# Eight experts in two interleaved streams: wide and narrow experts block by block in turn, instead of one after the other

## The chip, the cores and the metric

The kernel runs on one core of a Trainium2 chip. The metric is the device time of one execution in microseconds, the median of several runs. Beside it stands one profiled execution, whose trace all rows below come from.

## What is computed

The kernel is a two-layer backbone: layer 0 is a state-space and retention mixer with a dense feed-forward part, layer 1 is differential attention and a mixture of eight experts, of which each of the 256 tokens uses two. The change touches the experts alone:

```
def swiglu(h, w_gate, w_up, w_down):
    return (jax.nn.silu(h @ w_gate) * (h @ w_up)) @ w_down

def moe(h, w_router, w_gate, w_up, w_down):
    logits = (h @ w_router).astype(jnp.float32)
    top_val, top_idx = lax.top_k(logits, TOP_K)
    top_w = jax.nn.softmax(top_val, axis=-1)
    combine = jnp.sum(jax.nn.one_hot(top_idx, N_EXPERTS, dtype=jnp.float32) * top_w[..., None], axis=-2)
    out = jnp.zeros_like(h)
    for e in range(N_EXPERTS):
        out = out + combine[..., e:e + 1].astype(h.dtype) * swiglu(h, w_gate[e], w_up[e], w_down[e])
    return out
...
xl = xl + g2 * moe(hl, odd_router[j], odd_exp_gate[j], odd_exp_up[j], odd_exp_down[j])
```

The model width is 1024, an expert's inner width 3584, all in float32. One expert has 3 x 1024 x 3584 weights, 44 MB; the eight have 352 MB, and each weight is read once.

## The kernel before, in words

The experts are sorted by how many tokens chose them. The first four places have 128 token slots each and are called wide here; the last four have 64 slots and are called narrow (`SLOTS`). Tokens that fit nowhere would be done in a conditional part behind them, which this input doesn't enter. `ORDER` runs the places one whole expert at a time, wide and narrow in turn: 0, 7, 1, 6, 2, 5, 3, 4.

A *unit* is one weight transfer of 1 MiB (128 partitions x 2048 float32). An expert has 28 units of gate and up (seven blocks of 512 inner columns, four units each) and 14 units of down. `raw2` issues them on SP's queue in the order of the code, into a ring: two units go into four small buffers of 512 KB, the following ones into large tiles of two units each (`self.wide` lists the tiles: four of them before). A large tile is free again when both of its units have been used.

A **wide expert** (`expert`) splits each weight tile into a rounded part and a remainder: `wsplit` lets ScalarE make `hi` (L183) and VectorE make `lo` (L184), with three buffers of each, and each product is three matmuls (L194 to L196) on the whole 128x128 array. After each block come silu (L1493), the product with up (L1495), four transposes on TensorE (L1498), and the split of the result into `ah` and `al` (L1500, L1501). Its combine back to the tokens is L1522 and L1523.

A **narrow expert** (`expert_half`) multiplies the weights in plain float32, with no split. Its 64 slots fill half of the array's columns, and two halves of the weights' columns run side by side (L1443 gate and up, L1457 down; each such matmul has two records in the trace). After each block come silu (L1446), the product (L1448), and `turn`: two transposes (L1425) and a copy (L1426), which the code puts ahead of the third unit of the next block. Its end is a copy of the result scaled by the token's weight (L1465) and the combine (L1470).

`gather` fetches the slots of the next expert by matmuls with a selection matrix (L1357 and around), in the middle of the expert before it. `values_load` (L1245) reads the number of the expert at a place into a register of SP, since the address of its weights depends on it. In the last expert, a narrow one, the row of output gates (`row`, L357) and four partial sums on POOL (`so_far`, L1408 and L1409) are made, and `put` adds the last products and writes out.

The order on each engine is laid out when the program is built: a planner takes the instructions by their place in the code and by when it expects their operands and buffers. So an engine's order needn't be that of the code; at run time each engine keeps the order that it was given.

Of the kernel before, what the change touches and what calls it, by code (L numbers as in the profile page):

```python
# [10 lines left out]
F32 = mybir.dt.float32  # L11
# [8 lines left out]
P = 128  # L20
D = 1024
# [7 lines left out]

ORDER = (0, 7, 1, 6, 2, 5, 3, 4)  # L30
SLOTS = (CAP,) * 4 + (HALF,) * 4
# [108 lines left out]
class Net:  # L140
# [33 lines left out]
    def wraw(self, ap):  # L174
        t = self.pw.tile([P, 1024], F32, name="raw", tag="raw", bufs=5)
        self.nc.sync.dma_start(t, ap)
        return t
# [985 lines left out]
class Layer1Experts(Layer1):  # L1163
# [72 lines left out]
    def experts(self):  # L1236
        nc = self.nc
        v = nc.vector
        self.nraw, self.wide, self.al_slot, self.rest_slot = -5, (2, 3, 0, 1), 4, 4
        self.place, self.eid = self.rank, [0] * NE  # L1240
        g = self.gather(0, 0)
        self.sorted()
        for i, n in enumerate(ORDER):
            if n:
                self.eid[n] = nc.values_load(self.ids[0:1, n:n + 1], engines=[mybir.EngineType.SP],  # L1245
                                             min_val=0, max_val=NE - 1)
            nxt = ORDER[i + 1] if i + 1 < NE else None
            run = self.expert if SLOTS[n] == CAP else self.expert_half
            g = run(n, g, 0, nxt, not i, nxt is None)

        more = nc.values_load(self.more[0:1, 0:1], min_val=0, max_val=256)
        with self.tc.If(more > 0):
            self.nraw, self.wide, self.al_slot = 0, (3, 0, 1), 2
            for t in range(2):
                v.memset(self.moe[:, t, :], 0.0)
            for n in range(NE):
                extra = nc.values_load(self.extra[0:1, n:n + 1], min_val=-P, max_val=256)
                with self.tc.If(extra > 0):
                    self.expert(n, self.gather(n, SLOTS[n]), SLOTS[n], None, False, False)
# [69 lines left out]
    def gather(self, n, base):  # L1329
# [18 lines left out]
        for t in range(2):  # L1348
            nc.scalar.activation(pn[:, t, 0:w], p[:, t, 0:w], AF.Copy, scale=self.rs2[:, t:t + 1])
        xg = self.scr("q8", (P, KD, w)) if half else self.scr("q8", (P, 2, KD, P), F32R)  # L1350
        per = 512 // w
# [20 lines left out]
        for t in range(2):  # L1372
            nc.tensor.matmul(pt[:, 256:257], p[:, t, :], wts[:, t, n:n + 1], start=t == 0, stop=t == 1)
        pT = self.scr("m1", (P, 256), F32 if half else F32R)
        nc.scalar.activation(pT, pt[:, 0:256], AF.Copy)
        wt = self.scr("gw", (P, 1))
        v.tensor_copy(wt, pt[:, 256:257])
        return xg, pT, wt

    def raw2(self, ap):  # L1380
# [13 lines left out]
        self.nc.sync.dma_start(t.rearrange("p u c -> p (u c)"), ap)  # L1394
        return [t[:, i] for i in range(2)]
# [14 lines left out]

    def expert_half(self, n, gathered, base, nxt, first, final):

# [4 lines left out]
        sides = [slice(HALF * i, HALF * i + HALF) for i in range(2)]  # L1417
        if final:
            self.rest = self.big(self.rest_slot, (P, 3, D), name="rest")
            self.row("odd", 5, 0, self.rest[:, 2])  # L1420
        ap = self.big(5, (P, FE // P, HALF), name="ef")
        def turn(b, t):
# [7 lines left out]
        for b in range(FE // 512):  # L1430
            if final and 2 <= b < 6:
                self.so_far(b - 2)
# [27 lines left out]
        if final:  # L1460
# [5 lines left out]
        for t in range(2):  # L1466
            for j, s in enumerate(sides):
# [5 lines left out]
                else:  # L1473
                    v.tensor_tensor(self.moe[:, t, c], self.moe[:, t, c], pt, op=ALU.add)
        return out

    def expert(self, n, gathered, base, nxt, first, final):
        nc = self.nc
        v = nc.vector
        xg, pT, w_tok = gathered  # L1480
        ah = self.big(5, (P, FE // P, P), F32R, "eh")
        al = self.big(self.al_slot, (P, FE // P, P), F32R, "el")
        for b in range(FE // 512):
            pg, pu = self.mm(2 * (b % 2)), self.mm(2 * (b % 2) + 1)
            for u in range(0, KD, 2):
                raw = self.raw2(self.weights("exp_gu", n, b, u // 2))
                for i in range(2):
                    hi, lo = self.wsplit(raw[i])
# [6 lines left out]
            v.tensor_tensor(t, sg, pu, op=ALU.mult)  # L1495
            pt = self.tr()
            for f in range(4):
                nc.tensor.transpose(pt[:, P * f:P * f + P], t[:, P * f:P * f + P], self.ident)  # L1498
            p3 = pt.rearrange("p (f s) -> p f s", f=4)
            nc.scalar.activation(ah[:, 4 * b:4 * b + 4, :], p3, AF.Copy)  # L1500
            v.tensor_tensor(al[:, 4 * b:4 * b + 4, :], p3, ah[:, 4 * b:4 * b + 4, :].bitcast(F32), op=ALU.subtract)  # L1501
        out = self.gather(nxt, base) if nxt is not None else None
        py = [self.acc(), self.acc()]
        nd = FE // P
        for u in range(0, nd, 2):
# [3 lines left out]
            for f, j in sorted(steps, key=lambda s: s[1]) if u == nd - 2 else steps:  # L1509
                hi, lo = w[f - u]  # L1510
                c = slice(512 * j, 512 * j + 512)
                self.mm3(py[j], ah[:, f, :], al[:, f, :], hi[:, c], lo[:, c], f == 0, f == nd - 1)
        for j in range(2):
            c = slice(512 * j, 512 * j + 512)
# [4 lines left out]
            for t in range(2):  # L1519
# [4 lines left out]
                m = self.moe[:, t, c]  # L1524
                if first:
                    v.tensor_copy(m, pt)
                else:
                    v.tensor_tensor(m, m, pt, op=ALU.add)
        return out

# [18 lines left out]
```

## Time and profile before

| | us |
|---|---|
| median of 3 runs (2022.72 to 2029.66) | 2026.68 |
| the profiled execution | 2025.02 |
| span of its instructions | 2023.2 |
| first matmul of the first expert, from the span's start | 1120.5 |
| last weights landed | 2008.1 |

The profiled execution's own time is 1.8 us over its span. Times in the rows are microseconds from the span's start; a matmul's end is modelled, so the start of the next one says when it was done. PE is TensorE, PEld its weight loads, DVE VectorE, ACT ScalarE, POOL GpSimd and SP the engine whose queue issues the transfers. An idle time in brackets is that of the engine just before the instruction, with what ended it.

### The profile page before, as it was taken

The page shows a single profiled execution, that of the slowest core. Times are in us where ns is not written, and L with a number is a line of the kernel's source. Part 1 is how long each engine was busy: PE and PEld are TensorE (multiplying, and loading weights), DVE is VectorE, ACT ScalarE, POOL GpSimd, SP SyncE. Part 2 cuts the span into 40 slices and gives each one's busy share as a digit, 9 for nine tenths or more (in the row PEclk, how much of TensorE's full clock was granted, in tenths as well). Part 3 has the DMA queues.
Part 4 walks back from the last instruction along what each step waited for, and adds up shares of the span by engine and source line. Part 5 has one row for each costly group of instructions (what it writes and reads, how often), then busy time and mean ns, then how long its engine had stood idle before and what let it go on. Part 6 is the DMA issues. An engine that isn't in the chain of part 4 may idle for free.

```text
span 2023.2 us, 26554 instructions
## 1 busy us (share of the span) xinstructions
PE 1943.0 (96%) x9894; PEld 1440.6 (71%) x9894; DVE 1225.9 (61%) x2105; ACT 906.3 (45%) x1373; POOL 10.1 (1%) x12
## 2 busy tenths in 40 slices
PE   7999999999999999999989999999999999999997
PEld 4776778777888888877857887548854786558752
DVE  5568578745866565578566886049811984059700
ACT  5535346533333213245365774148712773158610
POOL 0000000000000000000000000000000000000010
PEclk9999999999999999999989999999999999999999
DMA  8333434442555554424325489999999999999897
GB/s 321 111 94 106 145 115 146 141 135 80 201 178 173 177 178 172 144 87 126 107 99 219 165 326 359 417 418 417 348 394 418 417 361 360 417 418 412 326 394 314
DMA packets 103865, 502.68 MB, mean 248 GB/s; under 512 B 13104, under 2 KB 13744, under 8 KB 69296
## 3 DMA queue, kind: packets, MB, share of 16 engines
q1 hardware_dynamic: 103728, 500.91, 66.0%
q8 instruction: 80, 1.31, 0.3%
q14 instruction: 57, 0.47, 0.1%
HBM read 495.62 MB, written 5.24 MB: 248 GB/s over the span
## 4 chain that ended last, share of the span: by engine, by line
PE 82%; DMA 7%; DVE 7%; ACT 3%; issue 1%; SPq 0%; ACTq 0%; DVEq 0%
PE mm L196 17%; PE mm L195 17%; PE mm L194 17%; PE mm L1443 9%; DMA wide<-exp_d 4%; PE acc L195 2%; PE acc L196 2%; PE acc L194 2%; DVE lo L184 2%; PE tr L1357 1%; PE acc L315 1%; PE acc L1457 1%; PE tr L1470 1%; PE mm L1138 1%; PE tr L817 1%
## 5 line engine op out<-in xcount | busy, mean ns | idle before, releaser
L183 ACT ACTIVATE hi<-raw 128x1024 fp32r<-128x1024 f32 x224 | 237.3, 1060 | 410.6 <-PE mm L196 204.7
L184 DVE TENSOR_TENSOR lo<-raw,hi 128x1024 fp32r<-128x1024 f32 x224 | 273.1, 1222 | 176.6 <-ACT hi L183 169.4
L184 DVE TENSOR_TENSOR lo<-wide,hi 128x1024 fp32r<-128x1024 f32 x268 | 324.7, 1223 | 34.8 <-ACT hi L183 14.1
L183 ACT ACTIVATE hi<-wide 128x1024 fp32r<-128x1024 f32 x268 | 282.5, 1061 | 75.2 <-PE mm L196 52.6
L195 PE MATMUL mm<-lo,q 128*128 128x512 f32 x448 | 177.8, 397 | 2.0 <-DVE lo L184 1.7
L196 PE MATMUL mm<-hi,q 128*128 128x512 f32 x448 | 176.0, 393 | 0.0
L194 PE MATMUL mm<-hi,hh 128*128 128x512 f32 x416 | 169.0, 407 | 1.7 <-DVE b L856 1.3
L1443 PE MATMUL mm<-wide,q 128*64 128x256 f32 x1424 | 168.7, 382 | 0.0
L195 PE MATMUL mm<-lo,hh 128*128 128x512 f32 x416 | 164.9, 396 | 0.0
L196 PE MATMUL mm<-hi,hl 128*128 128x512 f32 x416 | 163.9, 396 | 0.0
L194 PE MATMUL mm<-hi,q 128*128 128x512 f32 x448 | 159.1, 395 | 0.0
L194 PE MATMUL mm<-h2h,hi 128*128 128x512 f32 (+1 forms) x376 | 142.5, 379 | 1.3 <-ACT hi L183 1.3
L195 PE MATMUL mm<-h2l,hi 128*128 128x512 f32 (+1 forms) x376 | 141.9, 377 | 0.0
L196 PE MATMUL mm<-h2h,lo 128*128 128x512 f32 (+1 forms) x376 | 141.8, 378 | 0.0
L1443 PEld LDWEIGHTS mm<-wide,q 128*64 128x64 f32 x1424 | 100.3, 137 | 55.1 <-issue 8.1
L1448 DVE TENSOR_TENSOR s<-s,mm 128x256 f32<-128x256 f32 x28 | 11.8, 421 | 184.7 <-ACT s L1446 184.7
L195 PEld LDWEIGHTS mm<-lo,q 128*128 128x128 f32 x448 | 84.9, 190 | 24.1 <-DVE lo L184 4.1
L194 PEld LDWEIGHTS mm<-hi,q 128*128 128x128 f32 x448 | 84.5, 189 | 23.9 <-issue 4.5
L194 PEld LDWEIGHTS mm<-hi,hh 128*128 128x128 f32 x416 | 78.4, 189 | 27.8 <-issue 9.7
L196 PEld LDWEIGHTS mm<-hi,q 128*128 128x128 f32 x448 | 84.8, 189 | 16.9
L1457 PE MATMUL acc<-wide,ef 128*64 128x512 f32 x360 | 82.4, 598 | 11.0 <-DMA wide<-exp_d 11.0
L196 PEld LDWEIGHTS mm<-hi,hl 128*128 128x128 f32 x416 | 78.5, 189 | 17.1 <-issue 0.8
(393 smaller groups left out, 3319.7 us busy)
## 6 DMA issues: line engine op xcount, KB each, us to landing
wide<-exp_gu SPq DMA_DIRECT2D x177, 1024.0 KB, 10.4
wide<-exp_d SPq DMA_DIRECT2D x91, 1024.0 KB, 11.6
raw<-exp_gu SPq DMA_DIRECT2D x92, 512.0 KB, 12.5
raw<-odd_wmod SPq DMA_DIRECT2D x48, 512.0 KB, 4.0
raw<-w_in SPq DMA_DIRECT2D x44, 512.0 KB, 3.7
raw<-ffn_gu SPq DMA_DIRECT2D x44, 512.0 KB, 4.4
raw<-exp_d SPq DMA_DIRECT2D x42, 512.0 KB, 14.7
raw<-even_wmod SPq DMA_DIRECT2D x36, 512.0 KB, 3.7
```

Of the source, the lines that this page charges most:

```text
L183: nc.scalar.activation(hi, raw, AF.Copy)
L184: nc.vector.tensor_tensor(lo, raw, hi.bitcast(F32), op=ALU.subtract)
L194: mm(ps, lh, rh, start=first, stop=False, skip_group_check=skip)
L195: mm(ps, lh, rl, start=False, stop=False, skip_group_check=skip)
L196: mm(ps, ll, rh, start=False, stop=last, skip_group_check=skip)
L315: nc.tensor.matmul(ps[r:r + 32, :], self.cond[:, k, :], raw[:, 512 * kk:512 * kk + 512], start=k < 4, stop=k >= 4)
L817: nc.tensor.matmul(pe, m, r.rearrange("p h l -> p (h l)"), start=d + i == 0, stop=d + i == 2)
L1138: nc.tensor.matmul(ps, self.qT1[r, h, qs], self.kT1[r, h, :], start=True, stop=True)
L1357: nc.tensor.matmul(pt[:, w * kk:w * kk + w], self.x[:, 2 + t, P * (k + kk):P * (k + kk) + P], pn[:, t, 0:w], start=t == 0, stop=t == 1)
L1443: mm(ps[s, 256 * g:256 * g + 256], xg[:, k, :], raw[i][:, c:c + 256], start=k + g == 0, stop=k == KD - 1, skip_group_check=True)
L1457: mm(py[s], ap[:, f, :], raw[f - u][:, 512 * j:512 * j + 512], start=f == 0, stop=f == nd - 1, skip_group_check=True)
L1470: mm(pt, pT[s, P * t:P * t + P], y[s], start=True, stop=True)
```

## The change

`ORDER` goes. The wide places 0 to 3 and the narrow places 4 to 7 become two generators that yield after each block of gate and up and after each two units of down, 14 times an expert (`STEPS`). The wide stream runs three steps alone (`LEAD`), and then each loop turn asks one step of the wide and one of the narrow stream. The narrow stream gets operands of its own (`ef`, `xgh`, `pTs`) in the large tile 1, which leaves the ring: `self.wide` has three tiles instead of four. The narrow stream uses the PSUM banks 2 and 3, the wide stream 0 and 1 (and all four in its first three blocks). The narrow `turn` goes ahead of the second unit of its next block instead of the third; the wide transposes get a `turn` too, ahead of the second unit of the next block instead of right behind their own. The loads of expert numbers are ordered behind the weight transfer issued last. The gate row and the partial sums of the output come behind the wide stream's end.

```
-ORDER = (0, 7, 1, 6, 2, 5, 3, 4)
+STEPS, LEAD = 14, 3
...
     def wraw(self, ap):
-        self.nc.sync.dma_start(t, ap)
+        self.loaded = self.nc.sync.dma_start(t, ap)
...
     def experts(self):
-        self.nraw, self.wide, self.al_slot, self.rest_slot = -5, (2, 3, 0, 1), 4, 4
+        self.nraw, self.wide, self.al_slot, self.rest_slot = -5, (2, 3, 0), 4, 4
+        nb = self.big(1, name="nb")
+        self.ef = nb[:, 0:1792].rearrange("p (f s) -> p f s", s=HALF)
+        self.xgh = nb[:, 1792:2304].rearrange("p (k s) -> p k s", s=HALF)
+        self.pTs = [nb[:, 2304 + 256 * i:2560 + 256 * i] for i in range(2)]
         self.place, self.eid = self.rank, [0] * NE
         g = self.gather(0, 0)
         self.sorted()
-        for i, n in enumerate(ORDER):
-            if n:
-                self.eid[n] = nc.values_load(self.ids[0:1, n:n + 1], engines=[mybir.EngineType.SP],
-                                             min_val=0, max_val=NE - 1)
-            nxt = ORDER[i + 1] if i + 1 < NE else None
-            run = self.expert if SLOTS[n] == CAP else self.expert_half
-            g = run(n, g, 0, nxt, not i, nxt is None)
+        wide = [n for n in range(NE) if SLOTS[n] == CAP]
+        narrow = [n for n in range(NE) if SLOTS[n] == HALF]
+
+        def stream(run, ns, g):
+            for i, n in enumerate(ns):
+                if n:
+
+                    with self.tc.issue_after(self.loaded.ins):
+                        self.eid[n] = nc.values_load(self.ids[0:1, n:n + 1], engines=[mybir.EngineType.SP],
+                                                     min_val=0, max_val=NE - 1)
+                g = yield from run(n, g, ns[i + 1] if i + 1 < len(ns) else None, n == NE - 1)
+
+
+        full = stream(self.expert, wide, g)
+        for _ in range(LEAD):
+            next(full)
+        half = stream(self.expert_half, narrow, self.gather(narrow[0], 0))
+        for _ in range(STEPS * len(wide) - LEAD):
+            next(full)
+            next(half)
+        drain(full)
+        self.rest = self.big(self.rest_slot, (P, 3, D), name="rest")
+        self.row("odd", 5, 0, self.rest[:, 2])
+        for b in range(4):
+            self.so_far(b)
+        drain(half)
...
     def gather
-        xg = self.scr("q8", (P, KD, w)) if half else self.scr("q8", (P, 2, KD, P), F32R)
+        xg = self.xgh if half else self.scr("q8", (P, 2, KD, P), F32R)
...
-        pT = self.scr("m1", (P, 256), F32 if half else F32R)
+        pT = self.pTs[n % 2] if half else self.scr("m1", (P, 256), F32R)
...
     def expert_half
-            ps = self.mm(b % 4)
+            ps = self.mm(2 + b % 2)
             for u in range(0, KD, 2):
                 raw = self.raw2(self.weights("exp_gu", n, b, u // 2))
-                if t is not None and u == 4:
+                if t is not None and u == 2:
                     turn(b - 1, t)
...
             v.tensor_tensor(t, sg, ps[:, 256:512], op=ALU.mult)
-        out = self.gather(nxt, base) if nxt is not None else None
+            yield
         turn(FE // 512 - 1, t)
-        py = self.acc()
+        out = self.gather(nxt, 0) if nxt is not None else None
+        py = self.mm(3)
...
+            if u % 4 == 2 and u < nd - 2:
+                yield
...
     def expert
+        def turn(b, t):
+            pt = self.tr()
+            for f in range(4):
+                nc.tensor.transpose(pt[:, P * f:P * f + P], t[:, P * f:P * f + P], self.ident)
+            p3 = pt.rearrange("p (f s) -> p f s", f=4)
+            nc.scalar.activation(ah[:, 4 * b:4 * b + 4, :], p3, AF.Copy)
+            v.tensor_tensor(al[:, 4 * b:4 * b + 4, :], p3, ah[:, 4 * b:4 * b + 4, :].bitcast(F32), op=ALU.subtract)
+
+        t = None
         for b in range(FE // 512):
-            pg, pu = self.mm(2 * (b % 2)), self.mm(2 * (b % 2) + 1)
+
+            i0 = 2 * (b % 2) if not n and b < LEAD else 0
+            pg, pu = self.mm(i0), self.mm(i0 + 1)
             for u in range(0, KD, 2):
                 raw = self.raw2(self.weights("exp_gu", n, b, u // 2))
+                if t is not None and u == 2:
+                    turn(b - 1, t)
...
-            pt = self.tr()
-            for f in range(4):
-                nc.tensor.transpose(pt[:, P * f:P * f + P], t[:, P * f:P * f + P], self.ident)
-            p3 = pt.rearrange("p (f s) -> p f s", f=4)
-            nc.scalar.activation(ah[:, 4 * b:4 * b + 4, :], p3, AF.Copy)
-            v.tensor_tensor(al[:, 4 * b:4 * b + 4, :], p3, ah[:, 4 * b:4 * b + 4, :].bitcast(F32), op=ALU.subtract)
-        out = self.gather(nxt, base) if nxt is not None else None
+            yield
+        turn(FE // 512 - 1, t)
+        out = self.gather(nxt, 0) if nxt is not None else None
```

## Rows read from the trace of the kernel before

**Rows 1.** The page, part 1: busy time, share of the span, instructions.

```profile
PE 1943.0 (96%) x9894; PEld 1440.6 (71%) x9894; DVE 1225.9 (61%) x2105; ACT 906.3 (45%) x1373; POOL 10.1 (1%) x12
```

**Rows 2.** Table by stretches: length, busy time (instructions) by engine, clock, DMA share, GB/s.

```profile
1564.60:1691.20 126.60, 126.09 (x574) 102.39 (x573) 110.07 (x103) 94.63 (x105) 0.00 (x0) 0.99 0.97 388
1691.20:1789.50 98.30, 90.39 (x627) 47.20 (x626) 11.03 (x21) 15.35 (x35) 0.00 (x0) 1.00 0.98 397
...
1135.50:2008.10 872.60, 835.73 (x4672) 576.87 (x4672) 465.80 (x471) 422.48 (x530) 9.93 (x8) 1.00 0.97 386
...
1560.00:1580.00 20.00, 18.86 (x63) 11.80 (x62) 14.31 (x15) 12.51 (x14) 0.00 (x0) 0.91 1.02 418
1580.00:1600.00 20.00, 19.63 (x91) 15.91 (x90) 18.43 (x19) 15.39 (x18) 0.00 (x0) 1.00 1.01 418
```

**Rows 3.** Line 1457 in four stretches (as rows 2); then TensorE's timeline, one of them.

```profile
1308.16:1337.54 29.38, 25.80 (x112) 7.41 (x112) 1.00 1.01 417
1534.52:1560.43 25.91, 24.48 (x112) 7.82 (x112) 1.00 1.02 417
1759.76:1785.51 25.75, 24.69 (x112) 7.85 (x112) 1.00 1.02 417
1980.65:2011.81 31.16, 26.01 (x112) 7.49 (x112) 1.00 0.89 366
...
1759.76 12.24 PE L1457 MATMUL acc<-wide,ef 128*64 128x512 f32 x56
1771.82 3.60 PE L1457 MATMUL acc<-raw,ef 128*64 128x512 f32 x16
```

**Rows 4.** TensorE's timeline from 1565: start, length, line, operation, count, idle before.

```profile
1565.15 0.63 PE L195 MATMUL mm<-lo,q 128*128 128x512 f32 x1
1565.57 0.63 PE L196 MATMUL mm<-hi,q 128*128 128x512 f32 x1
1566.00 0.63 PE L195 MATMUL mm<-lo,q 128*128 128x512 f32 x1
...
1567.42 0.40 PE L196 MATMUL mm<-hi,q 128*128 128x512 f32 x1
1567.65 0.40 PE L194 MATMUL mm<-hi,q 128*128 128x512 f32 x1
```

**Rows 5.** A narrow expert's gate and up on TensorE; then who waited (us, times, longest).

```profile
1487.61 0.44 PE L1425 MATMUL tr<-con,s 128*128 128x128 f32 x2 [0.94 <-DVE s L1448]
1487.98 1.95 PE L1443 MATMUL mm<-wide,q 128*64 128x256 f32 x16
1489.76 3.62 PE L1443 MATMUL mm<-raw,q 128*64 128x256 f32 x32
...
PEld tr L1425 <- DVE s L1448: 31.5, 25, 1.5
```

**Rows 6.** TensorE's timeline where a wide expert's combine stands between narrow matmuls.

```profile
1247.01 1.08 PE L1443 MATMUL mm<-wide,q 128*64 128x256 f32 x8
1248.03 0.50 PE L1522 MATMUL tr<-s,m 128*128 128x512 f32 x1
1248.46 0.65 PE L1443 MATMUL mm<-wide,q 128*64 128x256 f32 x4
```

**Rows 7.** Line 1245: the loads of expert numbers, ns min/median/max, first and last start.

```profile
L1245 SPq TENSOR_LOAD <-order x7: 262/266/471, 1134.1 to 1141.5; - x7
```

**Rows 8.** POOL's groups by line: count, busy us, mean ns, idle before.

```profile
L1408 POOL TENSOR_TENSOR rest<-x,rest 128x512 f32<-128x512 f32 x4 | 5.1, 1276 | 1926.7 <-ACT rest L358 1926.7
L1409 POOL TENSOR_TENSOR rest<-rest,x 128x512 f32<-128x512 f32 x4 | 5.0, 1273 | 0.1
```

**Rows 9.** ScalarE's, then VectorE's timeline at the end of a narrow expert.

```profile
1560.43 0.69 ACT L1465 ACTIVATE s<-acc,gw 128x512 f32<-128x512 f32 x1 [25.41 <-PE acc L1457]
1561.01 1.99 ACT L183 ACTIVATE hi<-wide 128x1024 fp32r<-128x1024 f32 x2
...
1562.93 2.35 DVE L184 TENSOR_TENSOR lo<-wide,hi 128x1024 fp32r<-128x1024 f32 x2
```

More of the change, by code (lines that the diff above doesn't have):

```diff
@@ L1242, in experts @@
         self.sorted()
-        for i, n in enumerate(ORDER):
-            if n:
-                self.eid[n] = nc.values_load(self.ids[0:1, n:n + 1], engines=[mybir.EngineType.SP],
-                                             min_val=0, max_val=NE - 1)
-            nxt = ORDER[i + 1] if i + 1 < NE else None
-            run = self.expert if SLOTS[n] == CAP else self.expert_half
-            g = run(n, g, 0, nxt, not i, nxt is None)
+        wide = [n for n in range(NE) if SLOTS[n] == CAP]
[20 more added lines that the diff above has]
+        drain(half)
         more = nc.values_load(self.more[0:1, 0:1], min_val=0, max_val=256)
         with self.tc.If(more > 0):
-            self.nraw, self.wide, self.al_slot = 0, (3, 0, 1), 2
+            self.nraw, self.wide, self.al_slot = 0, (3, 0), 2
             for t in range(2):
@@ L1258, in experts @@
                 with self.tc.If(extra > 0):
-                    self.expert(n, self.gather(n, SLOTS[n]), SLOTS[n], None, False, False)
+                    drain(self.expert(n, self.gather(n, SLOTS[n]), None, False))
             for t in range(2):
@@ L1373, in gather @@
             nc.tensor.matmul(pt[:, 256:257], p[:, t, :], wts[:, t, n:n + 1], start=t == 0, stop=t == 1)
-        pT = self.scr("m1", (P, 256), F32 if half else F32R)
+        pT = self.pTs[n % 2] if half else self.scr("m1", (P, 256), F32R)
         nc.scalar.activation(pT, pt[:, 0:256], AF.Copy)
-        wt = self.scr("gw", (P, 1))
+        wt = self.scr("gwh" if half else "gw", (P, 1))
         v.tensor_copy(wt, pt[:, 256:257])
@@ L1393, in raw2 @@
             t = self.wide_raw[:, 2 * (k % 2):2 * (k % 2) + 2]
-        self.nc.sync.dma_start(t.rearrange("p u c -> p (u c)"), ap)
+        self.loaded = self.nc.sync.dma_start(t.rearrange("p u c -> p (u c)"), ap)
         return [t[:, i] for i in range(2)]
@@ L1409, in so_far, with expert_half @@
         pool.tensor_tensor(r, r, self.x[:, 2 + t, c], op=ALU.add)
-    def expert_half(self, n, gathered, base, nxt, first, final):
+    def expert_half(self, n, gathered, nxt, final):
         nc = self.nc
@@ L1417, in expert_half @@
         sides = [slice(HALF * i, HALF * i + HALF) for i in range(2)]
[L1418 to L1421, printed above, removed]
+        ap = self.ef
         def turn(b, t):
@@ L1430, in expert_half @@
         for b in range(FE // 512):
-            if final and 2 <= b < 6:
-                self.so_far(b - 2)
-            ps = self.mm(b % 4)
+            ps = self.mm(2 + b % 2)
             for u in range(0, KD, 2):
                 raw = self.raw2(self.weights("exp_gu", n, b, u // 2))
-                if t is not None and u == 4:
+                if t is not None and u == 2:
                     turn(b - 1, t)
@@ L1474, in expert_half, with expert @@
                     v.tensor_tensor(self.moe[:, t, c], self.moe[:, t, c], pt, op=ALU.add)
+        if not final:
+            yield
         return out
-    def expert(self, n, gathered, base, nxt, first, final):
+    def expert(self, n, gathered, nxt, final):
         nc = self.nc
@@ L1495, in expert @@
             v.tensor_tensor(t, sg, pu, op=ALU.mult)
-            pt = self.tr()
-            for f in range(4):
-                nc.tensor.transpose(pt[:, P * f:P * f + P], t[:, P * f:P * f + P], self.ident)
-            p3 = pt.rearrange("p (f s) -> p f s", f=4)
-            nc.scalar.activation(ah[:, 4 * b:4 * b + 4, :], p3, AF.Copy)
-            v.tensor_tensor(al[:, 4 * b:4 * b + 4, :], p3, ah[:, 4 * b:4 * b + 4, :].bitcast(F32), op=ALU.subtract)
-        out = self.gather(nxt, base) if nxt is not None else None
+            yield
+        turn(FE // 512 - 1, t)
+        out = self.gather(nxt, 0) if nxt is not None else None
         py = [self.acc(), self.acc()]
@@ L1512, in expert @@
                 self.mm3(py[j], ah[:, f, :], al[:, f, :], hi[:, c], lo[:, c], f == 0, f == nd - 1)
+            if u % 4 == 2 and u < nd - 2:
+                yield
         for j in range(2):
@@ L1524, in expert @@
                 m = self.moe[:, t, c]
-                if first:
+                if not n:
                     v.tensor_copy(m, pt)
@@ L1528, in expert @@
                     v.tensor_tensor(m, m, pt, op=ALU.add)
+        yield
         return out
```

## The prediction

> **What bounds the kernel now.** I read the page first: TensorE is busy 96% of the span [rows 1]. That is an average over stages, so the next view is the table by stretches, cut where the experts change. The reader is to see two unlike halves of one pair [rows 2]: a wide expert takes 126.6 us with VectorE busy 110 us and the DMA at 388 GB/s, below what it can move; a narrow one takes 98.3 us with VectorE nearly idle and the DMA at 397 GB/s. While a wide expert runs the DMA can also reach 418 GB/s, with VectorE at work (the row from 1580) [rows 2]. So the split of the weights doesn't slow the transfers, and 418 GB/s is what I use as their limit. From the first release of a buffer to the last landing (1135.5 to 2008.1) the mean is 386 GB/s: 336.8 MB in 872.6 us. At 418 GB/s they would take 805.8 us. That is 66.8 us of slack in the transfers, and it is the upper bound of what balancing can give.
>
> TensorE is the other limit, and what balancing gives is what TensorE stops waiting for. A busy share of 96% hides waits, since a matmul's end is modelled; so I took them from starts. They are three.
>
> *Weights not landed.* The down part of a narrow expert is 112 records of L1457. The four take 29.38, 25.91, 25.75 and 31.16 us [rows 3], and unhindered the records follow at 0.215 us (56 in 12.06 us, from 1759.76 to 1771.82 [rows 3]), 24.1 us for 112. The sum of what is over: 112.2 - 4 x 24.1 = 15.8 us.
>
> *A slower clock behind such a wait.* After the narrow expert that ends at 1560.4, wide matmuls start 0.43 us apart, 1565.57 to 1566.00, and then 0.23 us apart, 1567.42 to 1567.65 [rows 4]: the lower of the two levels, 1.2 GHz against 2.4 GHz, for some 3.8 us, in which 1.9 us are lost. The 20 us from 1560 have a mean granted clock of 0.91 for it [rows 2]. Two of the three changes from narrow to wide show this; I take 3.6 us for both.
>
> *The transposes of a narrow block.* L1425 waits for the product of its own block: 0.94 us of idle TensorE before 1487.61 [rows 5]. The weight loads name this wait 25 times, so 23.5 us. The code asks for these transposes two units into the next block, yet on TensorE they stand right behind their own block: the order on an engine is laid out when the program is built, by when operands are expected, and is not the code's.
>
> **The change, part by part.** The sum is made against the profiled execution, 2025.0 us (span 2023.2 and 1.8 us around it), which is 1.7 us under the median of 2026.7.
>
> *Two streams in turn.* A step holds 8 units of 1 MiB while both run gate and up, so TensorE has work whenever one stream's weights are late. I let the first two waits go: -15.8 and -3.6 us. Bounds: 0, if weights are still late, and -66.8 us if TensorE's needs were no limit at all.
>
> *Crossings between the streams.* This is the added cost. Where the combine of a wide expert already stands between narrow matmuls, eight narrow records from 1247.01 last until 1248.03, 1.02 us, where 16 of them take 1.78 us elsewhere (1487.98 to 1489.76), 0.89 us for eight: 0.13 us more. The single wide-shaped matmul that follows takes until 1248.46, 0.43 us, against a spacing of 0.23: 0.20 us more [rows 4 to 6]. There and back costs 0.33 us. The loop has 14 x 4 - 3 = 53 steps with both streams, so 53 x 0.33 = 17.5 us. Below: 0, if every crossing falls into a wait that stays anyway. Above: one crossing for each unit, up to four a step, 70 us. I take one a step, as the code has it.
> The Trainium skill, TensorEngine Tiling (Array Packing), section Tiling Modes, says that changing the tiling mode, and not just the tile, drains TensorE; wide matmuls use the whole array and narrow ones half its columns. The trace agrees, with the 0.33 us above. Without such a drain the sum below would be 17.5 us lower; the sum goes by the rows.
>
> *The narrow transposes, asked for at the second unit instead of the third, a wide block later.* They should find their product ready. But the row above says where they stood although the code asked otherwise: in the hole behind their block. Holes are still expected in the two-stream order, because a pair must load 84 units, 84 x 1.049 MB / 418 GB/s = 210.8 us, against a pair of 126.6 + 98.3 = 224.9 us that contains the waits above. I take the wait as staying: 0. Bounds: -23.5 us if the code's place holds, and more than 0 if what stands behind them also comes late (the second rival).
>
> *The wide transposes, one block later.* Their wait isn't seen now, since they already stand behind part of the next block; the narrow block covers them: 0.
>
> *Buffers.* The ring loses a 2 MiB tile to the narrow stream's operands: 2 units less are loaded ahead, 2 x 2.51 = 5.0 us of transfer. TensorE is the later one by the sum, so it is hidden; if the DMA were to set the end, it costs 5.0 us.
>
> *Gathers* stay 8 in number. *The ids of the experts*: seven loads to SP's registers, 0.27 us each [rows 7], now stand between DMA issues instead of all at the start. Queued behind each are SP's next weights; with about six units already asked for (the ring's eight less two in use), 15 us of transfer, this costs 0, and 7 x 0.47, the longest in the row, = 3 us at most. *The last expert's output row and four partial sums* move from inside the last narrow expert to behind the wide stream. POOL's eight operations take 10.2 us [rows 8]; the narrow stream has 6 units of down left, 48 records x 0.215 = 10.3 us, and the first output needs only the first quarter of the sums: 0, at most 3 us. *The first three wide blocks* run as now.
>
> Sum: 2025.0 - 15.8 - 3.6 + 17.5 = 2023.1; I predict 2023 us. That is no change that can be told: about 0.3%, 6 us, is what a measurement of this kernel can tell.
>
> **The rivals.**
>
> *The narrow transposes no longer wait.* For it: the code has a whole wide block between the product and its use, and where wide transposes have such cover TensorE doesn't wait. Against: the place they had before. 2023.1 - 23.5 = 1999.6 us.
>
> *The transfers set the end.* Crossings and waits fall where TensorE would wait for weights anyway, and the DMA runs at 418 GB/s throughout: 2025.0 - 66.8 + 5.0 = 1963 us. Against it: 224.9 us of a pair less the waits per pair (15.8 + 3.6 + 23.5 in four) is 214 us of TensorE, plus 4.4 us of crossings, above 210.8 us of transfer.
>
> *The split of the next wide block queues behind the narrow block* (slower). The place is ScalarE's queue. At 1560.43 ScalarE had idled 25.41 us before a narrow expert's last copy, and the two splits of the next wide weights, 1561.01, stood behind it; VectorE's part came at 1562.93, and the wide matmul that needs it began at 1565.15, 4.7 us after the copy [rows 4, 9]. In two streams each narrow gate-and-up block ends in such an operation (silu, then a product), 28 times. The price: some 0.3 us until the split can start behind the silu (0.58 behind the copy, which is twice as wide), 1.0 for ScalarE's part (1.99 for two), 1.2 for VectorE's (2.35 for two) [rows 9] and hand-overs of 0.2, together 2.7 us from the block's end to the first use, against 1.3 us in the sum (0.94 wait, 0.37 transposes [rows 5]), and two matmuls of 0.23 that need only ScalarE's part: about 1.0 us each, 28 us. The wide transposes would then fall inside narrow blocks, 28 further crossings of 0.33, 9 us: 2060 us. It decides from some ten such blocks on (10 us over the median, with its crossings). Against it: in a wide stretch the splits run ahead of the silu between them.
> The Trainium skill, Perfetto Trace Analysis, section Per-instruction lifecycle, says that ScalarE and VectorE take their instructions in strict order. The 25.41 us that ScalarE idled behind one waiting copy agree with it.
>
> *One crossing for each unit*: 2023 + 3 x 17.5 = 2076 us; nothing in the code asks for it, but the mixture at 1247 is that fine.
>
> **How the numbers follow.** Forecast 0.32; no wait at the transposes 0.30; the DMA's floor 0.05; splits queued 0.28; finer crossings 0.05. The forecast's own range is 2013 to 2033 (the 3 us terms, and half the transposes' waits gone). Cases of both signs hold most of the chance; for 8 in 10 the range reaches over the transposes' case, some 8 us beyond it, and over most of the split queue's (the early steps have full buffers, so its centre lies if anything below 2060): 1992 to 2065. Faster by over 0.3% (below 2020.6): 0.05 + 0.30 and a third of the forecast, 0.45. Within: the rest of the forecast but for its upper edge, 0.19. Slower: 0.28 + 0.05 and that edge, 0.36.
>
> **What would show it.** Right: the waits of L1457 for exp_d gone; 0.33 us around each change of stream; transposes of narrow blocks still after an idle 0.9 us; a DMA rate near 390 GB/s through the whole stage, without its ups and downs. The first rival: no idle before those transposes. The second: 418 GB/s throughout, and TensorE waiting for weights. The third: VectorE's split as the releaser of wide matmuls after narrow blocks, ScalarE idle before silu. I am wrong in the mechanism if TensorE waits for a PSUM buffer or for SP's issue, for which the trace of before gives no row.

## The result, and the profile after

The changed kernel takes 2118.87 us (median of 4 runs, 2117.91 to 2126.26); the kernel before, on the same chip, 2027.29 (2022.72 to 2029.66). The ratio is 1.046, with a 95% interval of 1.043 to 1.049: 92 us slower, 54 us beyond the upper end of the range. The prediction of 2023 us, no change that can be told, was wrong: the change costs time, clear of the noise. The profiled execution took 2118.55 us, its span is 2116.4 us. Lines of the changed file stand one to some forty lower than before: `hi` is now L184, `lo` L185, the wide matmuls L195 to L197, narrow gate and up L1464, narrow silu, product, transposes and their copy L1467, L1469, L1448 and L1449, the wide transposes and their split L1513, L1515 and L1516.

The page of the kernel after, part 1 (busy time, share of the span, instructions), answers to [rows 1]:

```profile
PE 1995.2 (94%) x9894; PEld 1456.5 (69%) x9894; DVE 1228.8 (58%) x2105; ACT 899.9 (43%) x1373; POOL 10.1 (0%) x12
```

TensorE is busy longer in all and a smaller share of the time, with the same 9894 instructions. The table by stretches, after, in the columns of [rows 2]: the stage of the experts, a stretch of early steps, and a stretch of steady ones:

```profile
1135.00:2000.00 865.00, 795.23 (x4193) 536.46 (x4192) 430.34 (x433) 384.29 (x491) 0.00 (x0) 0.96 0.91 351
1180.00:1210.00 30.00, 30.00 (x181) 21.86 (x181) 17.48 (x17) 14.68 (x18) 0.00 (x0) 1.00 1.01 405
1440.00:1460.00 20.00, 17.11 (x88) 12.44 (x86) 10.73 (x10) 9.50 (x11) 0.00 (x0) 0.91 0.93 355
```

In the stage the DMA moves 351 GB/s where it moved 386 before, and the granted clock fell from 1.00 [rows 2] to 0.96. The early steps have neither loss. What TensorE's matmuls waited for from 1112 us on, after, the five largest sums (us in total, times, longest):

```profile
PE mm L195 <- ACT hi L184: 21.1, 16, 1.6
PE tr L1448 <- DVE s L1469: 21.0, 23, 0.9
PE acc L195 <- ACT hi L184: 11.4, 8, 1.5
PE mm L196 <- DVE lo L185: 9.9, 19, 0.6
PE acc L196 <- DVE lo L185: 7.9, 12, 1.1
```

The waits for weights that the prediction let go [rows 3] are gone: no matmul waits for a transfer any more. Waits for a PSUM buffer, a sign that the prediction named for a mechanism it had not thought of, come to 3.1 us in 4 waits, all at the combines. In the place of the waits for weights stand waits for `hi` and `lo`, the two halves of the split. Where they come from is seen at the seam of one step. TensorE's, ScalarE's and VectorE's timelines, after, at the end of a narrow block (start, length, engine, line, operation, count, idle before and what ended it):

```profile
1442.14 0.44 PE L1448 MATMUL tr<-con,s 128*128 128x128 f32 x2 [0.94 <-DVE s L1469]
1444.00 0.73 PE L195 MATMUL mm<-hi,q 128*128 128x512 f32 x2 [1.42 <-ACT hi L184]
1445.26 0.79 PE L196 MATMUL mm<-lo,q 128*128 128x512 f32 x1 [0.53 <-DVE lo L185]
1445.85 0.63 PE L197 MATMUL mm<-hi,q 128*128 128x512 f32 x1
1446.28 0.63 PE L196 MATMUL mm<-lo,q 128*128 128x512 f32 x1
...
1448.35 0.39 PE L197 MATMUL mm<-hi,q 128*128 128x512 f32 x1
1448.58 0.40 PE L196 MATMUL mm<-lo,q 128*128 128x512 f32 x1
...
1438.50 0.60 ACT L1515 ACTIVATE eh<-tr 128x512 fp32r<-128x512 f32 x1 [4.91 <-PE tr L1513]
1441.25 0.38 ACT L1467 ACTIVATE s<-mm 128x256 f32<-128x256 f32 x1 [2.15 <-PE mm L1464]
1442.62 0.38 ACT L1449 ACTIVATE nb<-tr 128x256 f32<-128x256 f32 x1 [0.99 <-PE tr L1448]
1442.90 2.94 ACT L184 ACTIVATE hi<-wide 128x1024 fp32r<-128x1024 f32 x3
...
1441.66 0.42 DVE L1469 TENSOR_TENSOR s<-s,mm 128x256 f32<-128x256 f32 x1 [1.84 <-ACT s L1467]
1443.98 3.50 DVE L185 TENSOR_TENSOR lo<-wide,hi 128x1024 fp32r<-128x1024 f32 x3 [1.89 <-ACT hi L184]
```

The chain runs through three queues. TensorE ends the narrow block at 1441.20 (1442.14 less 0.94). ScalarE makes silu, VectorE the product, TensorE the transposes, ScalarE their copy; only then does ScalarE begin `hi` of the next wide weights, 1442.90, and VectorE `lo`, 1443.98. The first wide matmul that needs `lo` starts at 1445.26, 4.1 us after the narrow block's end. ScalarE idled 4.91, 2.15 and 0.99 us on the way; the splits were not late for want of time on ScalarE, they stood behind operations that waited. Then come wide matmuls 0.43 us apart until 1448.35, and after that 0.23, the two levels of the clock as in [rows 4].

The early steps, while the ring is still full, look otherwise. TensorE's timeline, after, in two early steps and at the transposes of the steady step ahead of the one above; then ScalarE's in an early step:

```profile
1187.40 1.95 PE L1464 MATMUL mm<-wide,nb 128*64 128x256 f32 x16
1189.28 0.44 PE L1448 MATMUL tr<-con,s 128*128 128x128 f32 x2
...
1208.46 0.44 PE L1448 MATMUL tr<-con,s 128*128 128x128 f32 x2
...
1418.12 0.44 PE L1448 MATMUL tr<-con,s 128*128 128x128 f32 x2 [0.94 <-DVE s L1469]
...
1192.64 1.04 ACT L184 ACTIVATE hi<-raw 128x1024 fp32r<-128x1024 f32 x1
1195.09 0.38 ACT L1467 ACTIVATE s<-mm 128x256 f32<-128x256 f32 x1 [1.41 <-PE mm L1464]
```

Here the transposes stand where the code asks for them, ahead of the second unit of the next narrow block, with no wait; a step lasts 19.2 us (1189.28 to 1208.46). On ScalarE the splits of the next wide weights stand ahead of silu, the last of them begun 2.45 us before it (1192.64 and 1195.09). In the steady state the splits stand behind silu and copy, the transposes stand behind their own block and a step lasts 24.0 us (1418.12 to 1442.14). So one program has both orders of the same code in it, and the difference between a clean step and a steady one is 4.8 us.

### The profile page after: what moved, and what is told of

It reads as the page before. It is cut to its first block, busy times and chain, and to the rows that moved or that the text cites. A ratio compares the mean times of both kernels' runs of the same rounds, so it can differ in the third digit from the quotient of the medians.

```text
span 2116.4 us, 26571 instructions
## 1 busy us (share of the span) xinstructions
PE 1995.2 (94%) x9894; PEld 1456.5 (69%) x9894; DVE 1228.8 (58%) x2105; ACT 899.9 (43%) x1373; POOL 10.1 (0%) x12
## 5 line engine op out<-in xcount | busy, mean ns | idle before, releaser
L184 ACT ACTIVATE hi<-raw 128x1024 fp32r<-128x1024 f32 x242 | 255.4, 1059 | 421.9 <-PE mm L197 217.2
L185 DVE TENSOR_TENSOR lo<-raw,hi 128x1024 fp32r<-128x1024 f32 x242 | 295.1, 1222 | 192.2 <-ACT hi L184 187.5
L185 DVE TENSOR_TENSOR lo<-wide,hi 128x1024 fp32r<-128x1024 f32 x250 | 300.7, 1223 | 121.0 <-ACT hi L184 111.9
L184 ACT ACTIVATE hi<-wide 128x1024 fp32r<-128x1024 f32 x250 | 257.7, 1056 | 120.8 <-PE acc L197 64.7
L196 PE MATMUL mm<-lo,q 128*128 128x512 f32 x448 | 185.0, 413 | 10.3 <-DVE lo L185 9.9
L197 PE MATMUL mm<-hi,q 128*128 128x512 f32 x448 | 181.8, 406 | 0.0
L195 PE MATMUL mm<-hi,q 128*128 128x512 f32 x448 | 161.2, 412 | 21.1 <-ACT hi L184 21.1
L195 PE MATMUL mm<-hi,hh 128*128 128x512 f32 x416 | 168.7, 407 | 1.7 <-DVE b L857 1.3
L197 PE MATMUL mm<-hi,hl 128*128 128x512 f32 x416 | 164.0, 396 | 0.0
L1464 PE MATMUL mm<-wide,nb 128*64 128x256 f32 x1344 | 157.1, 382 | 0.0
L195 PE MATMUL mm<-h2h,hi 128*128 128x512 f32 (+1 forms) x376 | 142.2, 378 | 1.4 <-ACT hi L184 1.4
L197 PE MATMUL mm<-h2h,lo 128*128 128x512 f32 (+1 forms) x376 | 141.1, 376 | 0.0
L1464 PEld LDWEIGHTS mm<-wide,nb 128*64 128x64 f32 x1344 | 94.3, 137 | 54.2 <-issue 10.0
L195 PEld LDWEIGHTS mm<-hi,q 128*128 128x128 f32 x448 | 85.9, 196 | 47.8 <-ACT hi L184 28.6
L196 PE MATMUL acc<-lo,eh 128*128 128x512 f32 x224 | 97.2, 434 | 7.9 <-DVE lo L185 7.9
L197 PEld LDWEIGHTS mm<-hi,q 128*128 128x128 f32 x448 | 88.5, 198 | 20.5 <-issue 2.3
L1469 DVE TENSOR_TENSOR s<-s,mm 128x256 f32<-128x256 f32 x28 | 11.8, 421 | 151.7 <-ACT s L1467 151.7
L195 PEld LDWEIGHTS mm<-hi,hh 128*128 128x128 f32 x416 | 78.5, 189 | 27.7 <-issue 8.9
L197 PE MATMUL acc<-hi,el 128*128 128x512 f32 x224 | 94.1, 420 | 0.0
## 6 DMA issues: line engine op xcount, KB each, us to landing
raw<-exp_d SPq DMA_DIRECT2D x56, 512.0 KB, 10.2
```

Of the source, the lines that this page charges most:

```text
L184: nc.scalar.activation(hi, raw, AF.Copy)
L185: nc.vector.tensor_tensor(lo, raw, hi.bitcast(F32), op=ALU.subtract)
L195: mm(ps, lh, rh, start=first, stop=False, skip_group_check=skip)
L196: mm(ps, lh, rl, start=False, stop=False, skip_group_check=skip)
L197: mm(ps, ll, rh, start=False, stop=last, skip_group_check=skip)
```

## The experiments

Each run is compared with the kernel before on the same chip; that kernel's median was 2024.76 us beside the first four runs, 2025.29 beside the next four and 2026.46 beside the last two. Differences below are to it.

### Only the narrow silu later

In the changed kernel silu and product of a narrow block are asked for after the next wide step, and ordered behind the third split of that wide block (`hi` on ScalarE, `lo` on VectorE), or the second split of the step where the wide stream is in its down part. The narrow transposes and their copy, which need the product, move back with them.

```
+            yield
+            with self.behind(*self.third):
                 sg = self.scr("s0", (P, 256))
                 nc.scalar.activation(sg, ps[:, 0:256], AF.Silu)
                 t = self.scr("s3", (P, 256))
                 v.tensor_tensor(t, sg, ps[:, 256:512], op=ALU.mult)
-            yield
```

> The two streams as in the changed kernel, but the narrow block's silu and product are traced one step later and ordered behind the third split of the next wide block on ScalarE and VectorE; the transposes follow from them. Queue theory (the wide splits wait behind silu, product, transposes and copy of the narrow block, 4.1 us from a narrow block's end to the first wide matmul with lo, and the clock falls after it; 28 such places): most of the 93 us go, 2025 to 2050 us, the rest staying because the wide transposes' copy still stands ahead of the splits where the narrow stream runs down. Crossing theory (the drain between the array's two tilings costs 1.7 us a step): no change, 2110 to 2120 us. Ring theory (the missing 2 MiB tile lets the transfers run dry): no change.

Measured: 2039.57 us (2037.29 to 2040.21), 14.8 over the kernel before, ratio 1.008 (1.006 to 1.010). Of 91.6 us, 76.8 are gone by moving silu and product, and with them the transposes and their copy, to later places in the queues.

### Only the wide transposes later

The transposes of a wide block, and with them their copy on ScalarE, ordered behind the second split and the last matmul of the next block's first unit. Silu stays where the change put it.

```
                 if t is not None and u == 2:
-                    turn(b - 1, t)
+                    with self.behind(*self.split, self.last_mm):
+                        turn(b - 1, t)
```

> The changed kernel with only the wide transposes (and with them their copy on ScalarE) behind the second split of the next block; the narrow silu stays where it was. If the two queues add up: 2119 - 26 = 2093 us. If the narrow silu holds the splits anyway: 2110 to 2119. If the wide copy was the larger part: under 2079.

Measured: 2079.72 us (2076.68 to 2087.65), 54.4 over before, ratio 1.026 (1.023 to 1.028): 37.2 us are gone, where 26 were expected (2093 us). What the edit doesn't name can move too, since the order is laid out anew: narrow transposes wait for their product 13 times in this run, 23 times in the changed kernel. Why the copy matters is seen in the changed kernel's timelines of ScalarE and TensorE where a narrow expert is in its down part:

```profile
1355.84 0.60 ACT L1515 ACTIVATE eh<-tr 128x512 fp32r<-128x512 f32 x1 [4.33 <-PE tr L1513]
1356.33 2.00 ACT L184 ACTIVATE hi<-wide 128x1024 fp32r<-128x1024 f32 x2
...
1355.25 0.55 PE L1513 MATMUL tr<-con,s 128*128 128x128 f32 x3
1357.43 0.73 PE L195 MATMUL mm<-hi,q 128*128 128x512 f32 x2 [1.63 <-ACT hi L184]
```

Narrow down has no silu, and yet the seam has its hole: the wide transposes stand behind the narrow matmuls, and the splits stand behind the copy of these transposes.

### Both later

The edits of the two runs above together.

> As e1_narrow_silu_late, and the wide block's transposes, copy and remainder are ordered behind the second split of the next wide block too. Queue theory: nothing that waits for TensorE stands ahead of the first splits any more; a step falls from 24.0 us to between 19.2 us (two steps with full buffers in the changed kernel) and 20.1 us (8 units at 418 GB/s), all in all 1990 to 2015 us, faster than the kernel before. Crossing theory: 2110 to 2120 us. Ring theory: 2110 to 2120 us, with weights as the releasers of TensorE.

Measured: 2013.84 us (2013.2 to 2014.57), 10.9 under the kernel before, ratio 0.995 (0.993 to 0.997). The two parts overlap: 76.8 and 37.2 alone, 102.5 together. TensorE's timeline of this version, ScalarE's, and its stage (here the narrow blocks are L1472, their transposes L1456, the copy of these L1457):

```profile
1428.51 1.95 PE L1472 MATMUL mm<-wide,nb 128*64 128x256 f32 x16
1430.39 0.44 PE L1456 MATMUL tr<-con,s 128*128 128x128 f32 x2
1434.27 1.90 PE L1472 MATMUL mm<-wide,nb 128*64 128x256 f32 x16
1436.09 0.73 PE L196 MATMUL mm<-hi,q 128*128 128x512 f32 x2
...
1449.60 0.44 PE L1456 MATMUL tr<-con,s 128*128 128x128 f32 x2
...
1430.87 0.38 ACT L1457 ACTIVATE nb<-tr 128x256 f32<-128x256 f32 x1 [1.83 <-PE tr L1456]
1432.38 2.00 ACT L184 ACTIVATE hi<-wide 128x1024 fp32r<-128x1024 f32 x2 [1.13 <-DMA wide<-exp_gu]
...
1135.00:2000.00 865.00, 849.13 (x4681) 568.49 (x4679) 462.52 (x468) 412.08 (x526) 9.90 (x8) 1.00 0.98 391
```

The step is 19.2 us (1430.39 to 1449.60), the same as a clean early step of the changed kernel; the transposes stand inside the next narrow block, the wide matmuls follow the narrow ones with no idle; the clock is at 1.00 and the DMA at 391 GB/s. The next splits begin at 1432.38, 3.7 us before the narrow block ends (1436.09), and what they wait for now is the landing of their weights. This version beats both kernels.

### The same buffers and places, one expert after another

The loop runs all steps of a wide expert, then all of a narrow one; the banks of the wide stream alternate over all four.

```
-        for _ in range(LEAD):
-            next(full)
...
+        for i in range(len(wide)):
+            for _ in range(STEPS):
+                next(full)
...
+            for _ in range(STEPS if i < 3 else 0):
+                next(half)
```

> All of the changed kernel's buffers, PSUM banks and places of the transposes, but each wide expert runs through before the next narrow one starts (the wide blocks take PSUM banks in pairs in turn again). Queue theory and crossing theory both: the interleave itself is what costs, so 2015 to 2040 us, near the kernel before. Ring theory, or one that blames the narrow stream's own buffers or the later transposes: it stays above 2080 us.

Measured: 2045.36 us (2044.06 to 2048.09), 20.6 over before, ratio 1.011 (1.009 to 1.013). That is 5 us above the range that was expected. So 71 of the 91.6 us come with the two streams being mixed, and some 20 with what the change altered besides.

### The kernel before with three tiles in the ring

```
-        self.nraw, self.wide, self.al_slot, self.rest_slot = -5, (2, 3, 0, 1), 4, 4
+        self.nraw, self.wide, self.al_slot, self.rest_slot = -5, (2, 3, 0), 4, 4
```

> The kernel before, with three large tiles in the ring of weights instead of four, nothing else. The one-by-one version with the changed kernel's buffers was 20.6 us over before. If the shorter ring is the cause: 2040 to 2048 us here. The prediction's term (two units less ahead, hidden, 5.0 us if not): 2025 to 2030. If the 20 us belong to the first change from wide to narrow in that version (its transfers fell to 226 GB/s from 1240 to 1280, against 375 before, 40 x (375 - 226) / 418 = 14 us): 2022 to 2028.

Measured: 2040.44 us (2039.02 to 2046.47), 15.2 over before, ratio 1.008 (1.005 to 1.011). The ring is most of the 20 us; the first change of streams, which I had blamed, is not. What TensorE waited for in this run (in the order of [rows 5]; L1457 is narrow down and L1443 narrow gate and up, as before):

```profile
PE acc L1457 <- DMA wide<-exp_d: 19.7, 27, 1.4
...
PE mm L1443 <- DMA wide<-exp_gu: 8.3, 12, 1.3
```

Narrow experts one at a time live on what lies in the ring when they begin. With a tile less their matmuls wait for weights in gate and up already, in each of the four, which in the kernel before they don't.

### The kernel before with the narrow transposes one unit later

The transposes of a narrow block ordered behind the matmuls of the next block's second unit, where the code of before asks for them.

```
                 if t is not None and u == 4:
-                    turn(b - 1, t)
+                    with self.tc.issue_after(last):
+                        turn(b - 1, t)
```

> The kernel before, with one thing changed: the narrow transposes are ordered on TensorE behind the second unit's matmuls, where the code asks for them. The prediction's term: 25 waits of 0.94 us go, 2004 us. If narrow experts wait for weights anyway, the waits only move to the weights and it stays at 2020 to 2030 us (blocks of 7.5 us for 4 units, where the transfers need 10.0 us).

Measured: 2023.21 us (2019.03 to 2027.37), ratio 0.999 (0.998 to 1.001). The wait of 0.94 us, 25 times [rows 5], is worth nothing when it is taken away. What TensorE's matmuls waited for in the kernel before:

```profile
PE tr L1425 <- DVE s L1448: 19.9, 21, 1.0
PE acc L1457 <- DMA wide<-exp_d: 11.0, 18, 1.4
```

And in this run (narrow down is L1458 in it, narrow gate and up L1444):

```profile
PE acc L1458 <- DMA wide<-exp_d: 18.2, 28, 1.4
PE mm L1444 <- DMA wide<-exp_gu: 4.1, 7, 1.4
...
PE tr L1425 <- DVE s L1449: 0.9, 1, 0.9
```

The 19 us that the transposes no longer wait are in part, 11.3 us, the waits for weights that come in their place (18.2 + 4.1 - 11.0); the time of the kernel didn't move at all, and where the rest went these rows don't say.

### Twice the crossings

The version with both later, with a yield after every two units of gate and up and after every unit of down.

```
-STEPS, LEAD = 14, 3
+STEPS, LEAD = 28, 6
...
+                if u == 2:
+                    yield
...
-            if u % 4 == 2 and u < nd - 2:
+            if u < nd - 2:
                 yield
```

> The version with both operations late, but with twice the steps, each of half the work: 106 crossings instead of 53. At the 0.33 us that the rows give for a crossing there and back: 2013.8 + 17.5 = 2031 us. If a crossing cost the 93 us of the change over 53 steps, 1.7 us: 2013.8 + 93 = 2107. If crossings fall into waits that stay: 2014.

Measured: 2045.85 us (2042.33 to 2046.89), 20.6 over before and so 31.5 over the version with both later: 0.59 us for each of the 53 more crossings that the code asks for, not 0.33, and far from 1.7. TensorE's timeline in it (narrow down is L1490):

```profile
1347.79 0.39 PE L198 MATMUL mm<-hi,q 128*128 128x512 f32 x1
1348.11 1.94 PE L1490 MATMUL mm<-wide,nb 128*64 128x512 f32 x8
1349.97 0.73 PE L196 MATMUL mm<-hi,q 128*128 128x512 f32 x2
1350.62 0.50 PE L197 MATMUL mm<-lo,q 128*128 128x512 f32 x1
1350.95 0.39 PE L198 MATMUL mm<-hi,q 128*128 128x512 f32 x1
```

From wide to narrow 0.32 us against the usual 0.23: 0.09. Eight narrow records to the next wide one 1.86 us against 8 x 0.215 = 1.72: 0.14. The first two wide ones 0.65 against 0.46: 0.19; the third 0.33 against 0.23: 0.10. That is 0.52 us at this crossing, and it is a dear one. Taken record by record from the timelines of this run and of the version with both later, the crossings with no wait behind them cost 0.36 to 0.37 us there and back (medians: 0.14 into the narrow stream, 0.22 to 0.23 out of it). And the engine's order has more of them than the code asks for: wide matmuls follow narrow ones 118 times in this run and 49 times in the version with both later, 69 more. At 0.36 us these are 25 of the 31.5 us; the rest isn't settled.

### The holes filled

The changed kernel, with six matmuls of a constant into a bank that nothing reads behind each narrow block's transposes; waits and queues stay.

```
+            with self.tc.issue_after(last):
+                idle = self.tr()
+                for i in range(6):
+                    mm(idle[sides[i % 2], 0:256], self.ident[:, 0:HALF], self.x[:, 2, 0:256], start=True, stop=True,
+                       skip_group_check=True)
```

> The changed kernel, with six extra matmuls of a constant (0.11 us a record, two records each, into a bank that nothing reads) behind each narrow block's transposes, 28 times; the waits stay as they are. If the lower clock behind the holes is a part of the loss of its own (0.04 of some 965 us, 38 us): a granted clock of 0.98 or more from 1135 to 2000 and 2119 - 38 = 2081 us, up to 2100 with those fillers that don't fall into a hole. If the time is set by the waits alone, whatever TensorE does in them: 2119 to 2137.

Measured: 2109.0 us (2106.93 to 2112.58), 83.7 over before, ratio 1.040 (1.038 to 1.043): 7.9 us gained, between the two expectations. The granted clock of the stage (1135 to 2000) is 0.99, against 0.96 in the changed kernel. TensorE's timeline where the filling (L1452) falls into the hole:

```profile
1450.52 0.44 PE L1448 MATMUL tr<-con,s 128*128 128x128 f32 x2 [0.94 <-DVE s L1474]
1450.89 1.52 PE L1452 MATMUL tr<-x,con 128*64 128x256 f32 x12
1452.38 0.73 PE L195 MATMUL mm<-hi,q 128*128 128x512 f32 x2
1453.64 0.50 PE L196 MATMUL mm<-lo,q 128*128 128x512 f32 x1 [0.53 <-DVE lo L185]
1453.98 0.40 PE L197 MATMUL mm<-hi,q 128*128 128x512 f32 x1
1454.21 0.40 PE L196 MATMUL mm<-lo,q 128*128 128x512 f32 x1
...
1473.12 0.44 PE L1448 MATMUL tr<-con,s 128*128 128x128 f32 x2 [0.94 <-DVE s L1474]
```

The first wide matmul starts 1.86 us after the transposes (1452.38 less 1450.52), as in the changed kernel (1444.00 less 1442.14), so the queue's delay is the same; but the wide matmuls then run 0.23 us apart from the second on (1453.98 to 1454.21), and the step takes 22.6 us (1450.52 to 1473.12) instead of 24.0. The lower clock costs 1.4 of the 4.8 us of such a step. Over the whole kernel the filling takes time of its own: 28 x 1.52 = 43 us, part of it spread between the matmuls of wide downs or inside a narrow block. How much of the 91.6 us is the clock's can't be read from this run.

### Other distances between the streams

`LEAD` 7 and `LEAD` 1 in the version with both later.

> The version with both operations late, with the narrow stream seven steps behind instead of three: a wide gate-and-up block (four units) then always stands beside two narrow units of down, and the other way round, six units a step; with three behind, steps hold eight, six and four. If what is left to gain is evenness (transfers at 391 GB/s on the mean from 1135 to 2000, 418 at best): up to 20 us less, 1994 to 2010. Against it, four more narrow steps run alone at the end, each two units (5.0 us of transfer) for 3.45 us of matmuls: about 6 us more, 2020, if evenness brings nothing.

> The same with the narrow stream one step behind: steps hold eight units or four, hardly any six. If evenness counts, the reverse of the run with seven: 2020 to 2035 us. If it doesn't: two narrow steps less alone at the end, 3 us less, 2011.

Measured: 2033.53 us for seven (2022.83 to 2039.43, ratio 1.002, 1.000 to 1.004), 2020.85 for one (2014.79 to 2026.89, ratio 0.998, 0.996 to 0.999). The run with one lies in the range that evenness gave, the run with seven speaks against it: its even steps brought no gain. Three steps have the lowest ratio of the three; against one step the intervals overlap (0.993 to 0.997 and 0.996 to 0.999). With seven, waits for `hi` in wide downs come back (10.2 us in 9 waits, against 2.0 in 2 with three steps), and seven narrow steps run alone at the end; which of them weighs more wasn't tried.

## Why the prediction was wrong

*Two streams in turn, -15.8 and -3.6.* The waits for weights did go. The slower clock didn't: it came back behind the new holes, 0.96 in the stage against 1.00. That mixing is good for the weights shows only once the queues are in order: the version with both later is 26 us faster than the kernel before with the same ring of three tiles (10.9 under and 15.2 over), crossings included.

*The split of the next wide block queues behind the narrow block.* This is what happened, and I had put it as the slower rival at 0.28; in the sum the queue had no term. The place was right: ScalarE's queue, then VectorE's, and then TensorE. The step that failed is leaving it out on the argument against it, "in a wide stretch the splits run ahead of the silu between them". That argument is from a stretch of one stream, in which silu waits for the same engine's work as the splits do; it says nothing of a queue in which silu waits for another stream's matmuls. The experiments with silu and copy moved show the cause: 102.5 us by order alone. With the order mended, what is left of the sum, -15.8 - 3.6 + 17.5 = -1.9 us, stands against a measured -10.9.

The price was wrong too: 28 x 1.3 = 37 us, against 91.6. I priced silu alone in front of the split, 2.7 us from the block's end to the first use. Measured are 4.1 us, since the transposes and their copy stand there as well, and the product between them; and the slow matmuls behind the hole, 1.4 us, had no term, although [rows 4] show such a stretch behind a hole in the kernel before. And only the 28 gate-and-up blocks were priced, while the seams at narrow downs have their hole too (1357.43).

*The wide transposes, 0.* This term failed as well. I asked whether TensorE would wait for their input and found cover. Their copy on ScalarE, a 0.60 us operation, stands ahead of the splits and waits 4.33 us for TensorE; moved without silu it gives 37.2 us, with silu already moved 25.7 (14.8 and 10.9).

*The narrow transposes, 0.* Right in that they went behind their own block, 23 times with a wait of 0.9 us. The bound "more than 0 if what stands behind them also comes late" was the case. The rival that valued their wait at 23.5 us (1999.6 us) would not have held in the kernel before either: taken away there, it gives nothing, and waits for weights grow in its place. Waits on one engine can't be added as gains while another limit lies just below.

*Crossings, 17.5.* About right for the 53 that the code asks for: 0.36 us each in the rows, against 0.33, is 19 us. The doubled run bounds it from above: 31.5 us over 69 more crossings is 0.46 each. What I missed is that the engine's order can hold more crossings than the code has steps. The Trainium skill, TensorEngine Tiling (Array Packing), section Tiling Modes, says only that a change of mode drains TensorE; the rows agree with a cost at each change, and part of it lies behind the change, at the first wide matmul (0.34 us against 0.23).

*Buffers, 0 or 5.0.* Mis-sized: a shorter ring costs 15.2 us in the kernel before. I priced the tile as bytes to be loaded later, 2 x 2.51 us; but the wait comes again with each narrow expert. What it costs in two streams wasn't measured.

*The transfers set the end, 1963.* Not reached: the stage had 391 GB/s in the version with both later and 396 with the narrow stream one step behind, with TensorE busy 849 and 850 of 865 us.

*Gathers, ids and output rows* were not tried by themselves; the 10.9 us that the version with both later gains leave no large loss there.

Why the planner put silu and the copies ahead of the splits in the steady steps and not in the early ones, I can't show. It fits that it expected weights later than they come once the ring is no longer full; no run here changed its expectation. The code asks for silu ahead of the next wide splits in all of them; the early steps show that the order on ScalarE needn't follow it.

## What to carry to other kernels

When two streams share an engine, read each queue in order and ask of every instruction what it waits for: one small operation that waits for stream A holds all of stream B behind it, however idle the engine is. The work that feeds the bound engine (here the splits) goes into the queue ahead of the work that drains it (silu, copies), by an explicit order where a planner would choose. Price such a seam by its whole chain, operation by operation through all queues until the bound engine runs at full clock again, and don't count a removed wait as a gain before asking which limit lies just below.

## What the runs showed of the hardware

Behind a hole of three pieces, 0.94, 1.42 and 0.53 us with matmuls between them, wide matmuls ran 0.43 us apart, at 1.2 GHz, until 1448.35, and the mean granted clock from 1440 to 1460 was 0.91. With 1.52 us of matmuls of a constant in the middle piece they ran 0.23 us apart, at 2.4 GHz, though the other two pieces remained. The Trainium skill, TensorE: Matmul & The Clock Gate, section Part 1: The HAM clock gate (the "warmup" mystery), says that activity releases the throttle; the filled hole agrees. The order of a few small operations in ScalarE's queue moved TensorE's clock as well as its waits: 0.96 with silu and copy in front, 1.00 with both behind.

A crossing between matmuls on the whole array and matmuls on half its columns cost 0.36 to 0.37 us there and back in the timelines of two versions, of which 0.09 to 0.10 us fall on the last matmul before each change and 0.11 us on the first wide one behind it.
